# A hybrid encoder layer with retrieved experts: stores moved to ScalarE's queue, a quota of gathered rows, and norms in parts

## The chip, the cores and the metric

One core of a Trainium2 chip runs the whole kernel as one program. The metric is device time in microseconds (us), the median of several executions; less is better. Times inside an execution come from one that was profiled.

## What is computed

One layer works on 1024 tokens of 1024 features. A mixer (an RG-LRU group and an S5 group side by side) is followed by a retrieval of experts, and this second half is what the change touches. The reference, cut to that half:

```python
q = (xb @ wq).reshape(128, 8, 256)              # per block of 128 tokens, 8 heads
s1, s2 = q[..., :128] @ k1.T, q[..., 128:] @ k2.T
v1, i1 = top_k(s1, 16); v2, i2 = top_k(s2, 16)
sc, cidx = top_k((v1[..., :, None] + v2[..., None, :]).reshape(128, 8, 256), 16)
e = i1[cidx // 16] * 128 + i2[cidx % 16]        # 128 experts of 16384 for each token
g = softmax(sc)
act = gelu(einsum('thkd,td->thk', u_tab[e], xb))
out = einsum('thk,thkd->td', g * act, v_tab[e])
h = h + out;  result = rms_norm(h, normf_g)
```

## The kernel before

Of the eight blocks of 128 tokens, three are *gathered* and five are *dense*.

For a **gathered block** (`gather`), each token's 128 expert rows are fetched by an indirect DMA that GpSimd issues. One instruction of VectorE handles one fetched row tile of 128 x 1024: 128 times a product with the block's input `xg` (u rows, which give `act`), then 128 times a multiply and add into `hb` (v rows). Three blocks make 768 rows. Eight row buffers (`rows`) hold what was fetched ahead. A block ends with `finish`, the final norm.

For the **dense blocks** every expert is used with a weight that is mostly zero. `build_g` makes those weights for one block after another: it selects the block's candidates (`topk`), then, in 32 groups of four tokens, multiplies one-hot matrices `ohA` and `ohB` on TensorE and copies the product into `gs` on ScalarE. Every eight groups a store of 2 MB puts `gs` into DRAM (`G_d`). `ahead` makes at the same time 97 of 128 tiles of first-layer activations: load `ur`, split it into a high part `uh` (ScalarE) and a low part `ul` (VectorE), 48 matmuls, Gelu into `aa`, a store into `A_d`. A planner (`Merge.run`) chooses by costs of its own which of these threads writes its next instructions; a scheduler then sets the order on each engine. The engines follow that order strictly. Rows are paced by `PACE`, the planner's us between two.

The **dense schedule** (`dense`) is written out by hand: 32 chunks of four expert tiles (`JC`). In each it makes one more first-layer tile (`first`, 48 matmuls), weighs the activations `hr` and `ha` by the weights (`gt` loaded, `gq` on ScalarE), splits them and the expert rows `vr`, and multiplies into five blocks' sums: 24 matmuls each for blocks 0 to 3 into PSUM pairs (`pair`, two buffers) that `add` takes into `acc`, and block 4 into `total`. `rows_of` places the gathered rows that are left into seven slots of a chunk. `last` does the last chunk's blocks 1 to 4 and their `finish`.

All loads and stores named here are issued by the SP queue, in order, except the row fetches.

Of the kernel before, what the change touches and what calls it, by code (L numbers as in the profile page):

```python
# [844 lines left out]
PACE = 2.0  # L845


def peer(tc, a, cst, pools, h, ss, mg):
# [220 lines left out]
    def build_g(b):  # L1069
# [13 lines left out]
        def flush():  # L1083
# [3 lines left out]
            if t4 % GT == GT - 4:  # L1087
                t0 = b * P + t4 + 4 - GT
                nc.sync.dma_start(G_d[:, :, t0:t0 + GT].rearrange("j p t q -> p j (t q)"),
                                  gs.rearrange("p j t q -> p j (t q)"))  # L1090
                mg.dma(GT * 64)
# [51 lines left out]
    def gate():  # L1143
        return (lambda: mg.units < share[0]) if share else None

    def gather(n):

        xg = gp.tile([P, D], F32, name="xg", tag="xg", bufs=1)
        nc.sync.dma_start(xg, X_d[n])
        act = gp.tile([P, P], F32, name="act", tag="act", bufs=1)  # L1150
        for k in range(P):
# [3 lines left out]
            mg.units += 1  # L1155
        hb = gp.tile([P, D], F32, name="hb", tag="hb", bufs=1)
# [10 lines left out]
        finish(ND + n, hb)  # L1167
        yield

    def finish(b, x):  # L1170
        sq = rows.tile([P, D], F32, name="sqf", tag="row")
        nf = rows.tile([P, D], F32, name="nf", tag="row")
        nc.sync.dma_start(nf, a["gf"].partition_broadcast(P))
        st = gp.tile([P, 3], F32, name="st", tag="st")
        S.activation(sq, x, AF.Square, accum_out=st[:, 0:1])
        rsqrt_cols(mg, st[:, 1:2], st[:, 2:3], st[:, 0:1], 1.0 / D)
        V.scalar_tensor_tensor(x, x, st[:, 2:3], nf, ALU.mult, ALU.mult)
        nc.sync.dma_start(out_v[:, b], x)
# [90 lines left out]
    mg.run([], until="ahead")  # L1269
    pools.close("pk2", "ppt")  # L1270
# [8 lines left out]
    share[:] = [0.0]  # L1279
# [102 lines left out]
    def split_u(c):  # L1382
        uh = pu.tile([P, 8, P], F32R, tag="uh", name="uh")
        ul = pu.tile([P, 8, P], F32R, tag="ul", name="ul")
        split_to(uh, ul, raw_u.pop(c))
        return uh, ul

    def dense():
# [26 lines left out]
        u = split_u(1)  # L1415
        load_v(1, 0)
        carry = None
        for c in range(nch):
# [5 lines left out]
            if more:  # L1424
# [3 lines left out]
                next(fs)  # L1428
            if carry:
                add(*carry)  # L1430
# [11 lines left out]
            if c + 2 < nch:  # L1442
                u = split_u(c + 2)
# [9 lines left out]
            if not more:  # L1453
                finish(0, acc[0])
# [41 lines left out]
    def last(now, pr):  # L1496

        for b in (2, 3, 4):
            p_ = pair() if b < 4 else total
            for jj, t in enumerate(now):  # L1500
                second(p_, b, t, b < 4 and jj == 0, jj == JC - 1)
            if b == 2:
                add(1, pr[1])
                finish(1, acc[1])
            else:
                add(b - 1, p0)
                finish(b - 1, acc[b - 1])
            p0 = p_
        add(4, total)
        finish(4, acc[4])  # L1510
# [84 lines left out]
```

## Time and profile before

| | us |
|---|---|
| median of 3 runs | 2805.51 (2804.67 to 2807.54) |
| the profiled execution | 2802.4 |
| its span, first to last instruction | 2800.6 |
| mean granted TensorE clock, share of full speed | 0.957 |

The span lies 1.8 us inside the profiled execution's time. The program has these stages by the trace: the mixer to about 430 us; queries and first selections to about 700; weights, first-layer tiles and rows to 1657; the dense schedule to about 2740; the last chunk and the norms to the end.

### The profile page before, as it was taken

The numbers are of one execution on the slowest core, as the hardware profiler recorded it, in microseconds if no ns is written. First come the engines' busy times: TensorE is split into PE (matmuls) and PEld (weight loads), VectorE is DVE, ScalarE is ACT, GpSimd is POOL, SyncE is SP. The second block draws the span as 40 slices with busy tenths as digits, with TensorE's granted clock in tenths as the row PEclk, the third lists the DMA queues.
The fourth block names the chain that finished last, engine by engine and source line by source line (L and its number), as shares of the span: only waits on it lengthen the run. The fifth ranks groups of instructions, "written<-read, shape, count | busy, mean of one in ns | idle before, by whom it ended". The sixth has DMA issues, their size and how long they took to land.

```text
span 2800.6 us, 40982 instructions
## 1 busy us (share of the span) xinstructions
PE 2557.1 (91%) x14719; PEld 2308.3 (82%) x14719; DVE 2359.7 (84%) x4536; ACT 1321.8 (47%) x2401; POOL 1145.1 (41%) x777
## 2 busy tenths in 40 slices
PE   6888899888899999999989949999989999999997
PEld 5765688888799899998989848888878888888885
DVE  7786535599999999989989838989988888899996
ACT  5355524322286583864846823344343334443332
POOL 0000000033274474865836624444545554455540
PEclk9998899999999999999999979999999999999998
DMA  4110315466699899998998988999888999999994
GB/s 165 26 30 25 125 56 175 131 225 198 234 356 392 289 385 334 329 399 284 394 328 304 400 293 295 326 327 331 324 300 324 337 330 328 334 335 325 328 334 135
DMA packets 302413, 762.50 MB, mean 272 GB/s; under 512 B 28801, under 2 KB 126401, under 8 KB 297089
## 3 DMA queue, kind: packets, MB, share of 16 engines
q0 software_dynamic: 110592, 402.70, 40.1%
q1 hardware_dynamic: 184736, 345.85, 35.2%
q10 hardware_dynamic: 6880, 11.33, 1.2%
q8 instruction: 116, 1.90, 0.3%
q14 instruction: 89, 0.72, 0.1%
HBM read 669.14 MB, written 89.46 MB: 271 GB/s over the span
## 4 chain that ended last, share of the span: by engine, by line
PE 57%; DVE 21%; DMA 11%; ACT 7%; issue 4%; ACTq 0%; SPq 0%; DVEq 0%
PE vp L146 24%; PE ap L146 12%; PE total L146 6%; DMA A_d<-aa 5%; ACT ohB L146 4%; PE qp L146 4%; DVE row L146 3%; PE wop L146 3%; DVE ix L146 2%; DVE oh L146 2%; DVE ul L146 2%; DVE v L146 2%; PE gp L146 2%; DMA ur<-in_uT_dram 2%; DVE hb L146 1%
## 5 line engine op out<-in xcount | busy, mean ns | idle before, releaser
L1128 POOL DMA_INDIRECT row<-in_peer_u_dram,idx x384 | 564.5, 1470 | 1045.5 <-DVE ix L146 549.6
L1128 POOL DMA_INDIRECT row<-in_peer_v_dram,idx x384 | 577.8, 1505 | 508.0 <-DVE hb L146 392.2
L146 PE MATMUL ap<-xDl,uh 128*128 128x320 f32 x2048 | 655.1, 320 | 42.8 <-ACT aa L146 21.6
L146 PE MATMUL ap<-xDh,ul 128*128 128x320 f32 x2048 | 649.7, 317 | 18.2 <-DVE ul L146 18.2
L146 PE MATMUL ap<-xDh,uh 128*128 128x320 f32 x2048 | 646.4, 316 | 0.0
L146 DVE SCALAR_TENSOR_TENSOR hb<-row,act,hb 128x1024 f32<-128x1024 f32 x384 | 491.7, 1281 | 7.8 <-DMA hb<-H_d 2.7
L146 DVE CUSTOM_DVE_ANT_0 row<-row,xg 128x1024 f32<-128x1024 f32 x384 | 458.6, 1218 | 6.0 <-DMA xg<-X_d 5.0
L146 PEld LDWEIGHTS ap<-xDl,uh 128*128 128x128 f32 x2048 | 392.0, 191 | 46.0 <-ACT aa L146 23.2
L146 PE MATMUL vp<-vl,hh 128*128 128x512 f32 x1024 | 400.3, 391 | 12.3 <-DVE h L146 10.0
L146 PEld LDWEIGHTS ap<-xDh,ul 128*128 128x128 f32 x2048 | 392.1, 191 | 23.0 <-DVE ul L146 21.6
L146 PE MATMUL vp<-vh,hl 128*128 128x512 f32 x1024 | 400.0, 391 | 0.0
L146 PE MATMUL vp<-vh,hh 128*128 128x512 f32 x1024 | 399.9, 391 | 0.0
L146 PEld LDWEIGHTS ap<-xDh,uh 128*128 128x128 f32 x2048 | 391.5, 191 | 0.0
L146 ACT ACTIVATE gq<-gt 128x640 f32<-128x640 f32 x128 | 175.1, 1368 | 352.0 <-DVE hr L146 334.1
L146 DVE TENSOR_TENSOR ul<-ur,uh 128x1024 fp32r<-128x1024 f32 x128 | 155.9, 1219 | 111.1 <-ACT uh L146 110.9
L146 PE MATMUL gp<-ohB,ohA 128*128 128x128 f32 x1280 | 211.8, 284 | 40.6 <-ACT gs L146 19.6
L146 PEld LDWEIGHTS vp<-vl,hh 128*128 128x128 f32 x1024 | 192.9, 188 | 53.9 <-DVE h L146 11.7
L146 PEld LDWEIGHTS gp<-ohB,ohA 128*128 128x128 f32 x1280 | 186.2, 194 | 51.6 <-ACT ohB L146 25.3
L146 PEld LDWEIGHTS vp<-vh,hh 128*128 128x128 f32 x1024 | 192.9, 188 | 40.4
L146 PEld LDWEIGHTS vp<-vh,hl 128*128 128x128 f32 x1024 | 192.9, 188 | 39.3
L146 ACT ACTIVATE aa<-ap 128x320 f32<-128x320 f32 x194 | 85.4, 442 | 276.2 <-PE ap L146 252.5
L146 ACT ACTIVATE ohB<-ohB,kt 128x128 f32<-128x128 f32 x480 | 205.4, 509 | 0.0
(419 smaller groups left out, 4545.8 us busy)
## 6 DMA issues: line engine op xcount, KB each, us to landing
ur<-in_uT_dram SPq DMA_DIRECT2D x128, 512.0 KB, 6.8
vr<-in_peer_v_dram SPq DMA_DIRECT2D x128, 512.0 KB, 6.5
G_d<-gs SPq DMA_DIRECT2D x20, 2048.0 KB, 26.8
gt<-G_d SPq DMA_DIRECT2D x32, 1280.0 KB, 9.8
A_d<-aa SPq DMA_DIRECT2D x97, 320.0 KB, 7.9
hr<-A_d SPq DMA_DIRECT2D x96, 320.0 KB, 5.8
wqr<-in_wq_dram SPq DMA_DIRECT2D x32, 512.0 KB, 4.1
S_d<-sc SPq DMA_DIRECT2D x64, 128.0 KB, 3.9
```

The source lines that it names most:

```text
L146: return fn(*args, **kw)
L1128: G.indirect_dma_start(out=r, out_offset=None, in_=a["peer_v" if at >= P else "peer_u"], in_offset=bass.IndirectOffsetOnAxis(ap=idx[n][:, ...
```

## The change

1. The weights' stores are issued by ScalarE instead of SP.
2. `PACE` is 2.2 instead of 2.0, and the rows stop at a `QUOTA` of 370 until the dense schedule begins. Before, 389 rows are done by then, so the dense schedule now holds 398 instead of 379.
3. The next gathered block's input `xg` is loaded as soon as this block's u rows are done, no longer at the next block's start.
4. `finish` comes in two parts, the squares and the scaling. For a gathered block, one row of the next block lies between them. In the tail the weights `nf` of the norm are loaded once for all five dense blocks, and a block's squares come before the scaling of the block ahead of it. Before, each block loaded its own and was normed in one go.
5. In a chunk, the copy `uh` of the tile for the next chunk but one is written before the second half of this chunk's activations instead of after the first block's matmuls (`high_u`); the difference `ul` stays where it was (`low_u`).

```diff
-PACE = 2.0
+PACE, QUOTA = 2.2, 370
...
-                nc.sync.dma_start(G_d[:, :, t0:t0 + GT].rearrange("j p t q -> p j (t q)"),
-                                  gs.rearrange("p j t q -> p j (t q)"))
+                nc.scalar.dma_start(G_d[:, :, t0:t0 + GT].rearrange("j p t q -> p j (t q)"),
+                                    gs.rearrange("p j t q -> p j (t q)"))
...
     def gate():
-        return (lambda: mg.units < share[0]) if share else None
+        return (lambda: mg.units < share[0]) if share else (lambda: mg.units < QUOTA)
+
+    xgs, pending = [], []
+
+    def load_x(n):
+        if n < NG:
+            xgs.append(gp.tile([P, D], F32, name="xg", tag="xg", bufs=1))
+            nc.sync.dma_start(xgs[n], X_d[n])
...
-        xg = gp.tile([P, D], F32, name="xg", tag="xg", bufs=1)
-        nc.sync.dma_start(xg, X_d[n])
+        if n == 0:
+            load_x(0)
+        xg = xgs[n]
...
             mg.units += 1
+            if pending:
+                pending.pop(0)()
+        load_x(n + 1)
...
-        finish(ND + n, hb)
-        yield
-
-    def finish(b, x):
-        sq = rows.tile([P, D], F32, name="sqf", tag="row")
+        pending.extend(finish(ND + n, hb, last_norm()))
+        pending.pop(0)()
+        yield
+
+    def last_norm():
         nf = rows.tile([P, D], F32, name="nf", tag="row")
         nc.sync.dma_start(nf, a["gf"].partition_broadcast(P))
-        st = gp.tile([P, 3], F32, name="st", tag="st")
-        S.activation(sq, x, AF.Square, accum_out=st[:, 0:1])
-        rsqrt_cols(mg, st[:, 1:2], st[:, 2:3], st[:, 0:1], 1.0 / D)
-        V.scalar_tensor_tensor(x, x, st[:, 2:3], nf, ALU.mult, ALU.mult)
-        nc.sync.dma_start(out_v[:, b], x)
+        return nf
+
+    def finish(b, x, nf):
+
+        st = gp.tile([P, 3], F32, name="st", tag="st", bufs=3)
+
+        def squares():
+            sq = rows.tile([P, D], F32, name="sqf", tag="row")
+            S.activation(sq, x, AF.Square, accum_out=st[:, 0:1])
+
+        def scaled():
+            rsqrt_cols(mg, st[:, 1:2], st[:, 2:3], st[:, 0:1], 1.0 / D)
+            V.scalar_tensor_tensor(x, x, st[:, 2:3], nf, ALU.mult, ALU.mult)
+            nc.sync.dma_start(out_v[:, b], x)
+        return [squares, scaled]
...
     mg.run([], until="ahead")
+    share[:] = [2 * NG * P]
...
-    share[:] = [0.0]
...
+            if c + 2 < nch:
+                uh = high_u(c + 2)
             if carry:
                 add(*carry)
...
             if c + 2 < nch:
-                u = split_u(c + 2)
+                u = low_u(c + 2, uh)
...
     def last(now, pr):
 
-        for b in (2, 3, 4):
-            p_ = pair() if b < 4 else total
+        while pending:
+            pending.pop(0)()
+        nf = last_norm()
+        parts = [finish(b, acc[b], nf) for b in range(ND)]
+        parts[0][0]()
+        p0 = pr[1]
+        for b in range(2, ND):
+            p_ = pair() if b < ND - 1 else total
             for jj, t in enumerate(now):
...
+            add(b - 1, p0)
+            parts[b - 1][0]()
+            parts[b - 2][1]()
             p0 = p_
-        add(4, total)
-        finish(4, acc[4])
+        parts[ND - 2][1]()
+        add(ND - 1, total)
+        parts[ND - 1][0]()
+        parts[ND - 1][1]()
```

How this moves instructions is seen in three places.

The SP queue before, in the third dense block's build: two of its stores (`G_d`) with the stores of first-layer activations (`A_d`) and the loads of expert tiles (`ur`) between them.

```order
L1089 DMA G_d_3227<-gs_11315 128x32x128
L1221 DMA A_d_3226<-aa_11575 128x640
L1183 DMA ur_12050<-in_uT_dram 128x1024
L1221 DMA A_d_3226<-aa_11700 128x640
L1183 DMA ur_12151<-in_uT_dram 128x1024
L1221 DMA A_d_3226<-aa_11823 128x640
L1183 DMA ur_12257<-in_uT_dram 128x1024
L1089 DMA G_d_3227<-gs_11663 128x32x128
```

ScalarE now, at the same store: the copies into `gs`, the store, and the one-hot matrices of the next group behind it.

```order
L146 ACTIVATE gs_11296<-gp_11599 128x4x32x4
L146 ACTIVATE aa_11559<-ap_11619 128x320
L1089 DMA G_d_3227<-gs_11296 128x32x128
L146 ACTIVATE ohB_11671<-iota_63,kt_10633 128x128 x3
L146 ACTIVATE ohB_11671<-ohB_11671,kt_10633 128x128 x3
L146 ACTIVATE uh_11712<-ur_11710 128x1024
```

The store stands between ScalarE's activations, and on SP only `A_d` and `ur` are left.

VectorE in the last dense block's build, before: the groups' one-hot matrices, a tile's low part `ul`, and gathered rows (`row,act<-row,xg`) between them.

```order
L146 TENSOR_TENSOR ul_15475<-ur_15472,uh_15474 128x1024
L146 TENSOR_TENSOR ohA_15536<-iota_63,kt_14760 128x512
L146 TENSOR_SCALAR ohB_15537<-iota_63,kt_14760 128x128
L146 ISA row_15383,act_12803<-row_15383,xg_12801 128x1024
L146 ISA act_12803 128x1
L146 TENSOR_TENSOR ohA_15559<-iota_63,kt_14760 128x512
L146 TENSOR_SCALAR ohB_15560<-iota_63,kt_14760 128x128
L146 ISA row_15422,act_12803<-row_15422,xg_12801 128x1024
```

VectorE in the same build now.

```order
L146 TENSOR_TENSOR ul_15064<-ur_15061,uh_15063 128x1024
L146 TENSOR_TENSOR ohA_15126<-iota_63,kt_14724 128x512
L146 TENSOR_SCALAR ohB_15127<-iota_63,kt_14724 128x128
L146 TENSOR_TENSOR ohA_15146<-iota_63,kt_14724 128x512
L146 TENSOR_SCALAR ohB_15147<-iota_63,kt_14724 128x128
L146 TENSOR_TENSOR ohA_15201<-iota_63,kt_14724 128x512
L146 TENSOR_SCALAR ohB_15202<-iota_63,kt_14724 128x128
L146 TENSOR_TENSOR ohA_15249<-iota_63,kt_14724 128x512
```

The rows between the groups are gone: this build and what follows it to the dense schedule hold 2 rows, and 61 before.

VectorE in the dense schedule where the second gathered block ends and the third begins, before: the last v row, the norm's small steps on `st`, its scaling, and the next block's first u row.

```order
L146 SCALAR_TENSOR_TENSOR hb_16273<-row_19128,act_12803,hb_16273 128x1024
L146 TENSOR_SCALAR st_19371<-st_19371 128x1
L146 RECIPROCAL st_19371<-st_19371 128x1
L146 TENSOR_TENSOR st_19371<-st_19371 128x1 x2
L146 TENSOR_SCALAR st_19371<-st_19371 128x1
L146 TENSOR_TENSOR st_19371<-st_19371 128x1
L146 SCALAR_TENSOR_TENSOR hb_16273<-hb_16273,st_19371,nf_19369 128x1024
L146 ISA row_19146,act_19384<-row_19146,xg_19382 128x1024
```

The same place now.

```order
L146 SCALAR_TENSOR_TENSOR hb_16700<-row_19377,act_12965,hb_16700 128x1024
L146 ISA row_19395,act_19622<-row_19395,xg_16698 128x1024
L146 ISA act_19622 128x1
L146 TENSOR_SCALAR st_19619<-st_19619 128x1
L146 RECIPROCAL st_19619<-st_19619 128x1
L146 TENSOR_TENSOR st_19619<-st_19619 128x1 x2
```

A u row of the third block has moved in between the last v row and the norm's steps, and the scaling follows further on.

## Rows read from the trace of the kernel before

**Rows 1.** The page's part 1: busy time of each engine, its share of the span, and its instructions.

```profile
PE 2557.1 (91%) x14719; PEld 2308.3 (82%) x14719; DVE 2359.7 (84%) x4536; ACT 1321.8 (47%) x2401; POOL 1145.1 (41%) x777
```

**Rows 2.** The busy time of each engine in stretches: bounds and length in us, then for each engine us busy and (instructions), then TensorE's granted clock as a share of full speed, the mean busy share of the 16 DMA engines, and GB/s. First the first four blocks' builds with the gaps behind them, then the first build, the gap behind it, and the last build.

```profile
778.50:1502.10 723.60, 673.79 (x4650) 660.66 (x4650) 685.84 (x1667) 469.41 (x1143) 439.80 (x280) 0.97 0.96 346
778.50:879.80 101.30, 94.84 (x667) 92.09 (x667) 94.58 (x172) 92.35 (x245) 72.59 (x50) 0.98 1.01 377
879.80:958.10 78.30, 73.84 (x505) 72.75 (x504) 78.30 (x282) 25.41 (x48) 27.71 (x23) 1.00 0.92 325
1502.10:1602.80 100.70, 93.99 (x672) 92.32 (x671) 92.86 (x169) 90.45 (x240) 71.27 (x49) 0.97 1.01 376
```

**Rows 3.** VectorE's waits from 778.5 to 1502.1 us: what waited, for what, us in total, times, the longest.

```profile
DVE ul L146 <- ACT uh L146: 28.0, 7, 11.0
DVE ohA L146 <- PE gp L146: 9.4, 4, 4.7
```

**Rows 4.** The SP queue in order of time around two of the weights' stores: start us, us, queue, line, DMA. The us are those that the issue itself takes.

```profile
1005.63 0.37 SPq L1089 DMA_DIRECT2D G_d<-gs  x1
1013.15 16.58 SPq L1221 DMA_DIRECT2D A_d<-aa  x1
1032.48 0.43 SPq L1089 DMA_DIRECT2D G_d<-gs  x1
1033.01 17.33 SPq L1221 DMA_DIRECT2D A_d<-aa  x1
```

**Rows 5.** The source line of the weights' stores: their count and the issue's ns (least, median, most), first and last start; then us from issue to landing.

```profile
L1089 SPq DMA_DIRECT2D G_d<-gs x20: 370/371/2082, 802.8 to 1611.3; - x20
DMA to landing us min/median/max: 16.7/26.8/37.7
```

**Rows 6.** ScalarE's own queue in the front part: seven loads that it issues, and the activation behind them.

```profile
284.58 7.25 ACTq L796 DMA_DIRECT2D h<-in_x_dram  x7
291.88 0.63 ACT L146 ACTIVATE wgh<-wg 128x512 fp32r<-128x512 f32 x1 [6.25 <-DMA wor<-in_w_out_dram]
```

**Rows 7.** VectorE in order of time, two gathered rows of the u kind one behind the other; then the page's part 5 for rows of the v and the u kind (count, us busy, mean ns).

```profile
1593.45 1.22 DVE L146 CUSTOM_DVE_ANT_0 row<-row,xg 128x1024 f32<-128x1024 f32 x1
1594.59 1.22 DVE L146 CUSTOM_DVE_ANT_0 row<-row,xg 128x1024 f32<-128x1024 f32 x1
L146 DVE SCALAR_TENSOR_TENSOR hb<-row,act,hb 128x1024 f32<-128x1024 f32 x384 | 491.7, 1281 | 7.8 <-DMA hb<-H_d 2.7
L146 DVE CUSTOM_DVE_ANT_0 row<-row,xg 128x1024 f32<-128x1024 f32 x384 | 458.6, 1218 | 6.0 <-DMA xg<-X_d 5.0
```

**Rows 8.** ScalarE, the SP queue and VectorE in order of time from the last copy of weights to the first product of the dense schedule.

```profile
1610.65 0.60 ACT L146 ACTIVATE gs<-gp 128x512 f32<-128x512 f32 x1 [0.45 <-PE gp L146]
1611.28 0.37 SPq L1089 DMA_DIRECT2D G_d<-gs  x1
1636.67 0.32 SPq L1265 DMA_DIRECT2D gt<-G_d  x1
1642.88 1.33 ACT L146 ACTIVATE gq<-gt 128x640 f32<-128x640 f32 x1 [17.70 <-DMA gt<-G_d]
1657.73 0.82 DVE L146 TENSOR_TENSOR hr<-hr,gq 128x640 f32<-128x640 f32 x1 [33.87 <-DMA hr<-A_d]
```

**Rows 9.** The chain of waits in the dense schedule, the start of three chunks one behind another (start us, us, what), and the busy time in the whole dense schedule and in one chunk.

```profile
1984.72 7.03 PE ap L146 x48
2019.00 7.04 PE ap L146 x48
2064.16 7.03 PE ap L146 x48
1676.00:2740.00 1064.00, 1055.68 (x5160) 909.64 (x5160) 946.17 (x1021) 423.39 (x463) 536.68 (x368) 0.99 0.91 325
1984.70:2019.00 34.30, 34.30 (x171) 29.57 (x170) 31.13 (x31) 13.81 (x15) 18.91 (x12) 1.00 0.89 319
```

**Rows 10.** VectorE in order of time in the chunk that begins at 2019.00, those instructions that it waited before, and TensorE's wait in the same chunk.

```profile
2027.49 1.23 DVE L146 TENSOR_TENSOR ul<-ur,uh 128x1024 fp32r<-128x1024 f32 x1 [2.96 <-ACT uh L146]
2032.64 0.16 DVE L146 RECIPROCAL st<-st 128x1 f32<-128x1 f32 x1 [1.36 <-ACT st L146]
2034.26 1.29 DVE L146 SCALAR_TENSOR_TENSOR hb<-hb,st,nf 128x1024 f32<-128x1024 f32 x1 [0.69 <-DMA nf<-in_gf_dram]
2040.54 1.22 DVE L146 CUSTOM_DVE_ANT_0 row<-row,xg 128x1024 f32<-128x1024 f32 x1 [4.99 <-DMA xg<-X_d]
2045.25 0.79 PE L146 MATMUL vp<-vl,hh 128*128 128x512 f32 x1 [8.30 <-DVE h L146]
```

**Rows 11.** VectorE's waits in the dense schedule, two of them.

```profile
DVE ul L146 <- ACT uh L146: 76.5, 29, 8.4
DVE hb L146 <- DMA hb<-H_d: 2.7, 1, 2.7
```

**Rows 12.** The tail: TensorE's last matmul, and three of VectorE's five scalings of a block.

```profile
2783.54 0.39 PE L146 MATMUL total<-vh,hh 128*128 128x512 f32 x1
2770.29 1.28 DVE L146 SCALAR_TENSOR_TENSOR h<-h,st,nf 128x1024 f32<-128x1024 f32 x1 [1.16 <-DMA nf<-in_gf_dram]
2776.80 1.28 DVE L146 SCALAR_TENSOR_TENSOR h<-h,st,nf 128x1024 f32<-128x1024 f32 x1 [1.48 <-DMA nf<-in_gf_dram]
2795.79 1.28 DVE L146 SCALAR_TENSOR_TENSOR h<-h,st,nf 128x1024 f32<-128x1024 f32 x1 [1.37 <-DMA nf<-in_gf_dram]
```

More of the change, by code (lines that the diff above doesn't have):

```diff
@@ L1380, in load_u, with high_u, low_u @@
             nc.sync.dma_start(raw_u[c], a["uT"][tile(c, 2).j])
-    def split_u(c):
+    def high_u(c):
         uh = pu.tile([P, 8, P], F32R, tag="uh", name="uh")
+        S.activation(uh, raw_u[c], AF.Copy)
+        return uh
+    def low_u(c, uh):
         ul = pu.tile([P, 8, P], F32R, tag="ul", name="ul")
-        split_to(uh, ul, raw_u.pop(c))
+        V.tensor_tensor(ul, raw_u.pop(c), uh.bitcast(F32), ALU.subtract)
         return uh, ul
@@ L1414, in dense @@
         weights(1)
-        u = split_u(1)
+        u = low_u(1, high_u(1))
         load_v(1, 0)
@@ L1452, in dense @@
             add(0, pr[0])
-            if not more:
-                finish(0, acc[0])
             rows_of(2)
@@ L1496, in last @@
     def last(now, pr):
-        for b in (2, 3, 4):
-            p_ = pair() if b < 4 else total
-            for jj, t in enumerate(now):
[L1501 to L1507, printed above, removed]
+        while pending:
[6 more added lines that the diff above has]
+            p_ = pair() if b < ND - 1 else total
+            for jj, t in enumerate(now):
+                second(p_, b, t, b < ND - 1 and jj == 0, jj == JC - 1)
+            add(b - 1, p0)
+            parts[b - 1][0]()
+            parts[b - 2][1]()
             p0 = p_
-        add(4, total)
-        finish(4, acc[4])
+        parts[ND - 2][1]()
+        add(ND - 1, total)
+        parts[ND - 1][0]()
+        parts[ND - 1][1]()
     with tc.manual_schedule():
```

## The prediction

> **What bounds the kernel now.** I read the page first, then the stretches by stage, then the waits in each. Over the span TensorE and VectorE are both near full [rows 1], so the average says little. By stage there are three regimes.
>
> From about 700 to 1645 us the kernel does three things at once. It makes the weights of five blocks; I call a *build* the 32 groups of one block, and a *gap* the selection of the next block's candidates up to its first group. It makes 97 tiles of first-layer activations, and it works off gathered rows. In a build the DMA engines are full (share 1.01, 377 GB/s) while VectorE has 6.7 us idle of 101.3. In a gap VectorE has none: 78.30 of 78.30 [rows 2]. Over the first four builds and gaps it is busy 685.8 of 723.6 us. Of the 37.8 idle, 28.0 is a `ul` waiting for its `uh`, and 9.4 a group waiting for TensorE [rows 3]. The `uh` is late because its transfer is: behind a weights' store the SP queue's next issue stands 16.58 and 17.33 us, and the tile loads stand behind that [rows 4].
>
> The dense schedule, 1676 to about 2740, belongs to TensorE. A chunk takes 34.3 us, TensorE is busy in all of it, and VectorE in 31.1 [rows 9]. One chunk stands out: from 2019.00 to 2064.16, 45.2 us.
>
> The tail is serial: the last block's norm ends 13.1 us after the last matmul [rows 12].
>
> **The change part by part.** *Pace and quota.* Rows finished before the dense schedule fall from 389 to 370. A plain reading saves 19 rows of VectorE, 22 us. The order says otherwise. Counted over the whole order, builds one to four and their gaps hold 49, 21, 47, 22, 48, 22, 47, 22 rows before (278) and 53, 29, 42, 33, 40, 41, 35, 45 now (318). The last build with what follows holds 61 before and 2 now. So the quota is used up before the last build, in which VectorE then has 32 groups and its tile splits and stands idle, and the four stages in which it was the fullest engine get 40 rows more. A row starts 1.14 us after the one before; a row of the v kind is 0.06 longer [rows 7], so I take 1.17. 40 x 1.17 = 46.8, and one `ul` less (1.14) makes 45.7. VectorE's work there becomes 685.8 + 45.7 = 731.5 us against 723.6 elapsed: longer by at least 8 even with no idle.
>
> *The stores on ScalarE.* What the SP queue lost behind a store is gone, so the tiles' loads come in time and I take the 28.0 us of waits on `uh` away. The 9.4 us stay: 740.9. If nothing of the 28.0 goes, it is 769. The issue itself now costs ScalarE its own time: 0.37 us each as on SP, 2.08 at the most [rows 5]. ScalarE was busy 92.35 of 101.3 us in a build [rows 2], so four issues (1.5 us, at most 8.3) fit into 9 us; without that cover they would be 7.4 us over all twenty.
>
> The rows are now bunched, too. The fourth gap has 45 rows (0.524 MB each), 9 tiles (0.852 MB in and out) and one store (2.1 MB): 33.3 MB, or 29.7 less the seven rows fetched ahead. At a build's 377 GB/s that is 79 us, and VectorE's 45 x 1.17 + 9 x 1.14 make 63. The third gap misses 7 in the same way. Bounds 0 and 23; I take 4, nearer to nothing, since the builds ahead of these gaps now move less than they could. Stages one to four: 745 us, **+21** (bounds +8 and +68).
>
> *The last build and the hand-over.* The last build is no longer VectorE's nor the DMA's, but TensorE was busy 93.99 of its 100.7 us [rows 2] with nine tiles in it, and now there are ten (7.03 us each [rows 9]), so little can go: -2 (bounds -4 and +5). The hand-over took 46.5 us, from the end of the last `gs` (1611.25) to the first `hr` (1657.73): the store 25.4 until the load of `gt` could start, then 6.2 to `gq`, then the copies behind `gq` on ScalarE, the last half tile and its way through DRAM [rows 8]. Now no row transfers lie beside the store: I take 16.7, the shortest landing seen [rows 5], -8.7. It starts behind one more `aa` copy, +2, and four copies instead of three stand behind `gq`, half a tile more, +3.5. Together -3 (bounds -8 and +5). Last build and hand-over: **-5**.
>
> *Next block's input ahead, norms in parts.* In the slow chunk VectorE waits for `uh`, then through the norm for ScalarE's squares and root, then for `nf`, then 5.0 us for `xg`; the add that frees a PSUM pair comes late and TensorE stands 8.30 us [rows 10]. Now `xg` has been there for 128 rows, a gathered row lies between squares and root, and `uh` is early; what is left, the root (1.36) and up to 1 us for `nf`, is well inside what the add has: it came 8.3 us late after 11 us of waits, so some 3 us pass unseen. The chunk falls back to 34.3: -10.9. On the other side the quota moves the change from u to v of the second block into the dense schedule. Its `hb` load stands on the SP queue behind the next `xg` load, and VectorE will wait for it; the same wait later is 2.7 us [rows 11], inside VectorE's 3.2 idle of a chunk, so I take +1 (up to +5). **-10**.
>
> *Late tile copied first.* `uh` is copied between the two halves of the activations. This takes away most of 76.5 us of VectorE idle in the dense schedule [rows 11], but TensorE did not wait for it: 0, with TensorE's 34.3 as cover. The same cover hides the 19 more rows (22 us over 31 chunks, 0.7 each, against 3.2 idle); without it they cost 22.
>
> *The tail.* Before, each block's cycle is 6.2 to 6.5 us, held by its own load of `nf`. Now `nf` is loaded once, squares go ahead of the earlier block's scaling, and TensorE's 24 matmuls of a block set the pace (5.4 us: a chunk without its 7.03 is 27.3 for 120). Following the new order with the old durations: last rows one row later (+1.2), scalings that end at about 2772.5 (that block's `nf` still follows the store of the gathered block), 2777.4, 2782.3 and 2784.9, and the last near 2790 against 2797.07: **-7** (bounds -4 and -9).
>
> **The sum.** +21 - 5 - 10 - 7 = -1. The profiled execution took 2802.4 us (span 2800.6), 3 us under the median of the runs, 2805.5; at the median's level the new kernel takes about **2804 us**: no change that can be measured (0.2%, 5.6 us, is about what a measurement of this kernel can tell).
>
> **The rivals.** *The store frees nobody* (slower, from the point at which less than about 20 of the 28 us go). The builds run at 377 GB/s with the engines full; what the tile loads lose to a store on their own queue they may lose to the same bytes on another. Then the 28.0 us stay, stages one to four cost +49, and the sum is +27: 2832; with half of it, 2818. For it: the share of 1.01 and tile loads that land late in every build. Against it: the SP issue itself stands still for 17 us, and three of four builds now carry 5 to 12 rows less.
> The Trainium skill (DMA: Bandwidth & Descriptors, section "Issuing engines are not separate DMA queues") says that starting DMAs from several engines saves only the sequencer's issue time, since all run on the same 16 engines. By that rule alone this rival would be right and the time 2832; the trace agrees in the full share and differs in the 17 us, which are sequencer time and far from small.
>
> *The last build runs free* (faster). If VectorE's idle vanishes altogether in the first four stages (+8), and the last store, alone on its queue and with no rows beside it, lands at once and lets the hand-over end at TensorE's own pace (-14 with the last build), the sum is 8 - 14 - 10 - 7 = -23: 2782. For it: TensorE has 4.5 tiles left after the last group, 32 us, and 46.5 pass. Against it: the chain store, load, copies, tile, store, load stays in series.
>
> *ScalarE held by the issue.* ScalarE's seven loads of `h` took 7.25 us to issue and its next activation began only at their end [rows 6], so an issue is ScalarE's own time. If the store holds it as long as SP's next issue stood, 17 us, twenty of them are 340 us, less 2.5 us each of slack: 3094. Against it: the stores' own issues read 0.37 on SP. It decides from 2.5 us an issue.
>
> *The dense wait moves.* If the early second block's `hb` or the split norm makes an add late, 8 of the 10 us come back: 2812.
>
> **How the numbers follow.** The sum with its own spread of 8 us: 0.46 (of it 0.14 faster, 0.27 same, 0.05 slower). The last build runs free: 0.25. The store frees nobody, wholly or by half: 0.18. ScalarE held: 0.04. The dense wait moves: 0.07 (0.04 same, 0.03 slower). Faster 0.39, same 0.31, slower 0.30. The range reaches to the free last build below and nearly to the whole 28 us above, 2782 to 2829; the likeliest case's own is 2796 to 2812.
>
> **What would show it.** The first four builds and gaps take 735 to 755 us instead of 723.6, with VectorE busy about 731; no wait of `ul` on `uh` over a few us there; a last build with VectorE under half busy; the first `hr` 10 to 20 us later than 1657.7. No chunk over 36 us in the dense schedule, though its rows are 398. A last scaling some 10 us after the last matmul or less. I am wrong if the stores do not free SP (waits on `uh` as before), if the first four stages end no later than now, or if a chunk other than the old one grows.

## The result and the profile after

The changed kernel takes **2837.99 us** (median of 4 runs, 2835.85 to 2842.74), against 2806.53 us (2804.67 to 2811.03) for the kernel before in the same comparison: ratio 1.0112, 95% interval 1.0093 to 1.0131. It is slower by 31 us. The prediction was no change, 2804, with a range to 2829. The profiled execution took 2842.7 us (span 2841.0), 40.4 more in span than the one before; it was the slowest of the four, so differences by stage below add up to more than 31.

The page of the changed kernel: part 1, and two rows of part 2 (busy tenths of VectorE and of the DMA engines, 40 slices of 71 us).

```profile
PE 2579.3 (91%) x14719; PEld 2332.9 (82%) x14719; DVE 2366.1 (83%) x4536; ACT 1327.0 (47%) x2401; POOL 1101.5 (39%) x777
DVE  7787535599999999998997427999989999899997
DMA  5010315366698998999889557999999999899994
```

The totals hardly moved against [rows 1]; VectorE has 6 us more. The slices show where they lie: in slices 23 and 24 (1562 to 1705 us), the last build and the hand-over, VectorE falls to 4 and 2 tenths and the DMA engines to 5 and 5. In the ten slices ahead of that both are at 8 or 9, but for VectorE's 7 in the last of them, which lies in the fourth gap.

The stretches of the changed kernel (columns as in [rows 2]): the first four builds and gaps together, the first build, the third gap, the fourth gap, the last build.

```profile
783.40:1560.60 777.20, 688.47 (x4616) 677.16 (x4615) 733.30 (x1744) 472.36 (x1137) 463.35 (x318) 0.93 0.95 345
783.40:904.80 121.40, 98.79 (x667) 96.22 (x667) 113.14 (x274) 92.53 (x242) 78.02 (x55) 0.90 0.96 355
1281.00:1360.90 79.90, 71.06 (x448) 70.00 (x446) 67.26 (x103) 25.64 (x42) 60.08 (x40) 0.91 1.00 380
1481.30:1560.60 79.30, 67.49 (x446) 66.16 (x444) 64.16 (x105) 22.03 (x38) 63.81 (x44) 0.97 1.03 400
1560.60:1663.40 102.80, 100.52 (x725) 100.26 (x726) 44.32 (x79) 95.09 (x248) 5.90 (x5) 0.97 0.56 185
```

The first four stages grew from 723.6 to 777.2 us. In them VectorE is busy 733.3 us, which is what the prediction had (731.5). But 43.9 us of idle stand beside it, where 13 were forecast. (Before, 37.8 stood there, so most of what the stages grew by is VectorE's added work, 47.5 us.) In the last build VectorE is busy 44.3 of 102.8 us, and the build is no shorter for it.

VectorE's waits in the first four stages of the changed kernel (columns as in [rows 3]).

```profile
DVE row L146 <- DMA row<-in_peer_u_dram,idx: 26.5, 30, 1.5
DVE ohA L146 <- PE gp L146: 8.1, 7, 4.2
DVE row L146 <- issue: 4.3, 2, 3.3
DVE hb L146 <- DMA row<-in_peer_v_dram,idx: 2.6, 1, 2.6
DVE ul L146 <- ACT uh L146: 0.7, 3, 0.3
```

The wait of `ul` for `uh`, 28.0 us in [rows 3], is gone, as forecast. A new one has its size: rows that wait for their own transfer, 26.5 us in 30 pieces. With 4.3 us where GpSimd's issue came late and 2.6 for v rows that makes 33.4. Of these, 27.8 lie in the third and fourth gaps.

Two other things changed in these stages. The copies into `gs`, which never waited for a store before, now do:

```profile
ACT gs L146 <- DMA G_d<-gs: 26.5, 4, 13.0
```

And TensorE's granted clock is 0.93 on average there, 0.97 before. Both would reach VectorE as a wait for TensorE's products. That wait is 8.1 us here (and 1.3 more for TensorE's first-layer work), and it was 9.4 before, so neither shows as a cause of the longer stages.

ScalarE and VectorE from the last copy of weights to the first product of the dense schedule, in the changed kernel.

```profile
1668.29 0.60 ACT L146 ACTIVATE gs<-gp 128x512 f32<-128x512 f32 x1 [1.31 <-PE gp L146]
1668.91 0.37 ACTq L1089 DMA_DIRECT2D G_d<-gs  x1
1702.64 0.83 DVE L146 TENSOR_TENSOR hr<-hr,gq 128x640 f32<-128x640 f32 x1 [21.15 <-DMA hr<-A_d]
```

From the end of the last `gs` (1668.88) to the first `hr` (1702.64) are 33.8 us; it was 46.5 [rows 8].

The dense schedule of the changed kernel: its stretch; VectorE's wait for `hb` in it; one of the two such waits; TensorE's waits in the same chunk.

```profile
1702.60:2829.40 1126.80, 1097.87 (x5326) 943.82 (x5327) 1017.77 (x1120) 449.53 (x498) 558.14 (x390) 0.99 0.89 323
DVE hb L146 <- DMA hb<-H_d: 13.9, 2, 7.0
1769.43 2.60 DVE L146 SCALAR_TENSOR_TENSOR hb<-row,act,hb 128x1024 f32<-128x1024 f32 x2 [7.03 <-DMA hb<-H_d]
1775.87 0.50 PE L146 MATMUL vp<-vl,hh 128*128 128x512 f32 x1 [2.47 <-DVE h L146]
1780.88 0.50 PE L146 MATMUL vp<-vl,hh 128*128 128x512 f32 x1 [2.00 <-DVE h L146]
```

From the first product of block 4 to that of the next chunk the old slow chunk took 44.1 us (45.2 by its first tile, [rows 9]) and takes 36.8 now. But two other places grew. Where a block goes from u rows to v rows VectorE stands 7.0 us for `hb`, and TensorE waits for the adds behind it: two chunks there take 75.2 us instead of 68.6, and later two take 72.8.

TensorE's last matmul and VectorE's last scaling in the changed kernel.

```profile
2829.64 0.39 PE L146 MATMUL total<-vh,hh 128*128 128x512 f32 x1
2835.86 1.28 DVE L146 SCALAR_TENSOR_TENSOR h<-h,st,nf 128x1024 f32<-128x1024 f32 x1
```

The norm ends 7.5 us after the last matmul starts, against 13.5 [rows 12].

By stage (us; from first group to first group, so that the four stages before read 722.8; the tail from the last matmul's start):

| | first group starts | stages 1 to 4 | last build and hand-over | first `hr` to last matmul | tail |
|---|---|---|---|---|---|
| before | 778.5 | 722.8 | 156.4 | 1125.8 | 13.5 |
| after | 783.4 | 777.2 | 142.0 | 1127.0 | 7.5 |
| difference | +4.9 | **+54.4** | **-14.4** | +1.2 | -6.0 |

The first column is not the change's: nothing before it was edited to take time, and in the twelve kernels below it lies between 777.2 and 786.5 where that part is in the scheduler's order (the two in written order: 804 and 805).

### The profile page after: what moved, and what is told of

Read it like the earlier page. It is cut to its first block, busy times and chain, and to the rows that moved or that the text cites. A ratio compares the mean times of both kernels' runs of the same rounds, so it can differ in the third digit from the quotient of the medians.

```text
span 2841.0 us, 40982 instructions
## 1 busy us (share of the span) xinstructions
PE 2579.3 (91%) x14719; PEld 2332.9 (82%) x14719; DVE 2366.1 (83%) x4536; ACT 1327.0 (47%) x2401; POOL 1101.5 (39%) x777
## 5 line engine op out<-in xcount | busy, mean ns | idle before, releaser
L1128 POOL DMA_INDIRECT row<-in_peer_u_dram,idx x384 | 536.3, 1397 | 1185.8 <-PE qp L146 542.2
L1128 POOL DMA_INDIRECT row<-in_peer_v_dram,idx x384 | 562.3, 1464 | 461.8 <-DVE hb L146 322.8
L146 PE MATMUL ap<-xDh,ul 128*128 128x320 f32 x2048 | 662.2, 323 | 53.3 <-DVE ul L146 49.8
L146 PE MATMUL ap<-xDl,uh 128*128 128x320 f32 x2048 | 664.0, 324 | 30.1 <-ACT uh L146 20.2
L146 PE MATMUL ap<-xDh,uh 128*128 128x320 f32 x2048 | 655.6, 320 | 0.0
L146 DVE SCALAR_TENSOR_TENSOR hb<-row,act,hb 128x1024 f32<-128x1024 f32 x384 | 491.5, 1280 | 20.9 <-DMA hb<-H_d 13.9
L146 PEld LDWEIGHTS ap<-xDh,ul 128*128 128x128 f32 x2048 | 400.2, 195 | 60.1 <-DVE ul L146 58.9
L146 PEld LDWEIGHTS ap<-xDh,uh 128*128 128x128 f32 x2048 | 399.4, 195 | 0.0
L146 PE MATMUL gp<-ohB,ohA 128*128 128x128 f32 x1280 | 220.3, 288 | 42.7 <-DVE ohB L146 23.4
L146 PEld LDWEIGHTS gp<-ohB,ohA 128*128 128x128 f32 x1280 | 198.1, 201 | 49.5 <-issue 19.5
L146 PEld LDWEIGHTS vp<-vl,hh 128*128 128x128 f32 x1024 | 193.2, 189 | 54.4 <-DVE h L146 12.4
L146 PEld LDWEIGHTS vp<-vh,hh 128*128 128x128 f32 x1024 | 192.9, 188 | 40.4
L146 DVE TENSOR_TENSOR h<-h,vp 128x1024 f32<-128x1024 f32 x128 | 155.8, 1217 | 49.2 <-PE vp L146 49.0
```

Source lines behind the costliest of these rows:

```text
L146: return fn(*args, **kw)
L1128: G.indirect_dma_start(out=r, out_offset=None, in_=a["peer_v" if at >= P else "peer_u"], in_offset=bass.IndirectOffsetOnAxis(ap=idx[n][:, ...
```

## Experiments

Each kernel's ratio is to the kernel before on the same chip, in brackets its 95% interval. VectorE's order is given by its rows in build, gap, build, gap and so on; before: 49, 21, 47, 22, 48, 22, 47, 22, and 61 in the last build and behind it; after: 53, 29, 42, 33, 40, 41, 35, 45, and 2.

### One part at a time

**The stores alone** (`e1_stores`), on the kernel before:

```diff
-                nc.sync.dma_start(G_d[:, :, t0:t0 + GT]
+                nc.scalar.dma_start(G_d[:, :, t0:t0 + GT]
```

> The kernel before with the twenty stores of the weights begun by ScalarE and nothing else changed. Theory 1 (the stores' new engine changes the order on VectorE: 27, 30, 39 and 43 rows in the four gaps instead of 21, 23, 23 and 22, the next block's selection in the builds): the first four builds and gaps end 45 to 60 us later than before (723.6), with 20 to 40 us of VectorE idle on arriving rows, the hand-over is some 10 us shorter, and the kernel is slower by 30 to 45 us, about 2840. Theory 2 (the pace and the quota of rows did it; the stores alone only free the SP queue): faster by 15 to 30 us, about 2780.

**Pace and quota alone** (`e2_rows`), on the kernel before:

```diff
-PACE = 2.0
+PACE, QUOTA = 2.2, 370
...
-        return (lambda: mg.units < share[0]) if share else None
+        return (lambda: mg.units < share[0]) if share else (lambda: mg.units < QUOTA)
```

> The kernel before with the pace of 2.2 and the quota of 370 rows, and nothing else changed; the stores stay on SP. Theory 1 (the stores' engine made the new order): the gaps hold 19 to 21 rows, the order of the first four stages stays as before, they take 705 to 725 us, and the kernel is faster by 0 to 15 us, 2790 to 2805. Theory 2 (pace and quota bunch the rows and starve the last build): slower by 20 us or more, 2825 or over.

**The edits of the dense schedule and the tail alone** (`e3_dense`): the changed kernel with the stores on `nc.sync`, `PACE = 2.0` and no quota.

> The kernel before with the edits of the dense schedule and the tail alone (late tile copied first, norms in parts, next block's input ahead); stores on SP, pace 2.0, no quota. Both theories: the front part as before to within 5 us. The tail gives 6 us. With 389 rows ahead the second block goes from u to v before the dense schedule, so only the third block's wait for its hb is left, 4 us, and the old slow chunk gives back 7 to 11: faster by 9 to 13 us, about 2795. If the dense edits are worth nothing (what the slow chunk loses comes back elsewhere), about 2800.

**All but pace and quota** (`e4_no_rows`): the changed kernel with `PACE = 2.0` and no quota.

> The changed kernel with pace 2.0 and without the quota: stores on ScalarE, dense edits, 389 rows ahead. Theory 1 (the stores' engine): no better than the changed kernel within 10 us, 2828 to 2848. Theory 2 (pace and quota): the gain of stores and dense edits together, 2770 to 2790.

| | median, us | ratio | stages 1 to 4 | last build and hand-over | dense |
|---|---|---|---|---|---|
| stores alone | 2850.16 | 1.0157 (1.0127 to 1.0188) | 774.9 | 140.4 | 1126.3 |
| pace and quota alone | 2787.71 | 0.9926 (0.9900 to 0.9952) | 702.9 | 145.0 | 1141.2 |
| dense and tail alone | 2789.71 | 0.9925 (0.9896 to 0.9953) | 722.1 | 155.8 | 1114.9 |
| all but pace and quota | 2830.65 | 1.0074 (1.0046 to 1.0101) | | | 1112.4 |

(In the last one the fifth block's first group stands only 14 us behind the fourth build, so the cut by groups doesn't fall where it does in the others.)

Stores alone: the four stages, then VectorE's waits in them.

```profile
784.60:1559.50 774.90, 682.94 (x4616) 672.76 (x4614) 736.19 (x1749) 471.89 (x1137) 475.37 (x319) 0.94 0.95 348
DVE row L146 <- DMA row<-in_peer_u_dram,idx: 24.6, 30, 4.0
DVE ul L146 <- ACT uh L146: 0.6, 1, 0.6
```

Pace and quota alone: the same.

```profile
783.50:1486.40 702.90, 666.73 (x4642) 658.22 (x4642) 677.07 (x1651) 467.84 (x1139) 421.22 (x272) 0.98 0.97 349
DVE ul L146 <- ACT uh L146: 12.0, 6, 5.0
DVE ohA L146 <- PE gp L146: 13.6, 8, 5.9
```

Theory 2, which was the prediction's own (the quota bunches the rows and empties the last build), fell. The stores on ScalarE do it alone. Their order is 55, 27, 46, 30, 42, 39, 38, 43, and 19 behind, with the selection of the next block written into the builds; the quota then takes most of what is left for the last build. Pace and quota with the stores on SP leave the order nearly as it was (49, 19, 45, 21, 46, 21, 50, 20, and 49), take 9 us of VectorE's work and 16 of its waits on `uh` out of the four stages, and gain 20 us, though the dense schedule is 15 longer with them. Of the 42 us that the stores cost, 52 lie in the four stages (VectorE 736.2 busy instead of 685.8; 24.6 waiting for rows stand where 28.0 on `uh` stood), 16 come back in the last build and the hand-over, and 6 lie ahead of the change. The dense edits gain more than expected, 18 us by the medians; the profile has 11 in the dense schedule and 4 in the tail.

The parts do not add up: 42 - 20 - 18 would be 4, and the change costs 31. Stores and dense edits do add up (22.5 measured, 24 by the parts). What does not add up is pace and quota: they gain 20 us with the stores on SP, and with the stores on ScalarE they cost some 10 (1.0112 with them, 1.0074 without, intervals that overlap a little). The stretches show why: from the first group to the first `hr` of the changed kernel, then the same and the dense schedule without pace and quota.

```profile
783.40:1702.60 919.20, 820.28 (x5544) 808.19 (x5543) 781.29 (x1825) 578.03 (x1404) 469.24 (x322) 0.94 0.89 320
784.80:1702.90 918.10, 816.19 (x5545) 804.07 (x5543) 804.42 (x1859) 579.27 (x1405) 493.62 (x341) 0.94 0.92 333
1702.90:2815.30 1112.40, 1092.42 (x5328) 940.51 (x5328) 994.15 (x1081) 449.13 (x497) 526.52 (x371) 0.99 0.88 318
```

With the stores on ScalarE, 19 rows less ahead of the dense schedule bring nothing there (919.2 and 918.1 us): the rows that pace and quota take away are those of a last build in which VectorE has time. The cost is in the dense schedule, 1126.8 us with them and 1112.4 without. It is there with the stores on SP as well, 1141.2 against 1125.8 for the kernel before, where the gain ahead of it is larger. With the quota, the second gathered block goes from u to v rows inside the dense schedule; VectorE waits for `hb` twice there, 13.9 us, and once, 3.2, without.

### Is it the queue or the order?

**Stores begun by GpSimd** (`e5_pool`): `nc.gpsimd.dma_start(G_d...`, on the kernel before. The order on VectorE stays nearly that of before.

> The kernel before with the twenty stores begun by GpSimd instead of SP. VectorE's order stays nearly that of before (47, 46, 47, 47 rows in the builds and 23, 23, 23, 22 in the gaps). Theory 1a (a store on another queue than SP is good; what costs is the order that comes with ScalarE): the 28 us of ul waiting for uh shrink under 8, the first four builds and gaps take 695 to 715 us, 2780 to 2800. Theory 1b (a store off SP is itself the cost, since its bytes now lie beside the tiles' loads or the gs buffers come free late): no gain or slower, 2808 to 2845. A third way: GpSimd's issue holds up the gathered rows behind it; then VectorE waits for rows, and the gain is gone too.

2811.34 us, ratio 1.0027 (1.0009 to 1.0046). The four stages and three of VectorE's waits in them:

```profile
779.00:1511.20 732.20, 680.45 (x4640) 667.75 (x4639) 686.67 (x1666) 470.64 (x1139) 455.63 (x295) 0.97 0.94 341
DVE row L146 <- DMA row<-in_peer_u_dram,idx: 20.7, 9, 6.7
DVE hb L146 <- DMA row<-in_peer_v_dram,idx: 19.6, 10, 4.8
DVE ul L146 <- ACT uh L146: 1.1, 1, 1.1
```

Then, in order of time, a store issued by GpSimd and the wait on VectorE behind it, twice:

```profile
989.75 1.74 POOL L1089 DMA_DIRECT2D G_d<-gs  x1
1006.51 1.29 DVE L146 SCALAR_TENSOR_TENSOR hb<-row,act,hb 128x1024 f32<-128x1024 f32 x1 [4.37 <-DMA row<-in_peer_v_dram,idx]
1017.11 1.74 POOL L1089 DMA_DIRECT2D G_d<-gs  x1
1034.02 1.28 DVE L146 SCALAR_TENSOR_TENSOR hb<-row,act,hb 128x1024 f32<-128x1024 f32 x1 [3.40 <-DMA row<-in_peer_v_dram,idx]
```

This is the third way of the expectation, with a turn. The wait on `uh` fell from 28.0 to 1.1 us, but VectorE waits 40.3 us for rows, and the longest of these waits end 16 to 18 us after a store was issued, 16.8 and 16.9 in these rows. That is about the time by which the SP queue's next issue stood still before: 16.58 and 17.33 us [rows 4], and 9.7 to 20.4 behind the twenty stores. In the changed kernel no issue on SP takes 5 us in these stages. So what comes next in the queue that holds a store waits for it: tile loads on SP, gathered rows on GpSimd. The issue itself is also dearer there, 1.74 us instead of 0.37. The run changes more than the queue, though: by part 3 of the pages GpSimd's stores go in 10560 packets, and in 82240 for the same bytes from SP or ScalarE.

**Written order, stores on SP and on ScalarE** (`e7_written_sp`, `e8_written_act`). From the first build to the last tile the scheduler is switched off, so that the engines follow the planner's order; VectorE, TensorE and GpSimd then have the same rows in both kernels.

```diff
     mg.add([(0.0, build()), (1.0, ahead())])
+    fixed = ExitStack()
+    fixed.enter_context(tc.manual_schedule())
     mg.run([], until="k")
...
     mg.run([], until="ahead")
+    fixed.close()
```

> The kernel before, from the first build to the last tile of activations in the written order of the program (no reordering of instructions there); stores on SP. Only a base for the next run: 51 to 52 rows in each build, 18 to 19 in each gap, the selection all in the gaps. Somewhere between 2790 and 2850. Waits of ul on uh behind the stores as in the kernel before, 20 us or more.

> As the run in written order, but the stores begun by ScalarE. The order of VectorE, TensorE and GpSimd is the same row for row, so the difference of the two is that of the queue alone. Theory 1a (the order made the loss): faster than the run with SP by 5 to 30 us. Theory 1b (a store on ScalarE costs by itself: gs copies that wait for a store that lands late, 26 to 41 us in the runs so far): slower than it by 15 us or more.

3500.29 us with SP, 3464.50 with ScalarE. The ranges do not overlap (3496.63 to 3505.51, 3461.43 to 3467.01). VectorE's wait in the four stages, first with SP, then with ScalarE:

```profile
DVE ul L146 <- ACT uh L146: 537.4, 59, 18.1
```

```profile
DVE ul L146 <- ACT uh L146: 496.9, 59, 14.6
```

The same four stages, first with SP, then with ScalarE:

```profile
805.00:2098.80 1293.80, 802.87 (x4680) 782.84 (x4679) 736.78 (x1665) 480.04 (x1141) 371.26 (x279) 0.78 0.59 194
803.80:2057.40 1253.60, 807.16 (x4680) 786.89 (x4679) 737.12 (x1666) 480.10 (x1141) 370.11 (x279) 0.80 0.61 200
```

With the order held, the stores on ScalarE are worth 36 us (5 to 30 were expected), and the wait of `ul` is 40 us shorter. So in this order the queue is not the cost. But this order is not the scheduler's. The kernel with SP was expected at 2790 to 2850 us and both are far slower, with builds of 200 us and the DMA engines busy 0.59 and 0.61 of the time. So the 36 us are not what a tuned order would gain, and the pair does not show what a store on ScalarE's queue costs where the DMA engines are full; no copy into `gs` waits for a store here. For the scheduler's order the changed kernel's own rows speak: the wait on `uh` is gone, the wait for TensorE has not grown, and the 47.5 us of added work are the order's. Whether the rows' waits of 33.4 us come from the order alone stays open, since no run holds the scheduler's order with the stores on ScalarE.

The Trainium skill (DMA: Bandwidth & Descriptors, section "Issuing engines are not separate DMA queues") has it that starting DMAs on several engines saves sequencer time alone. Here the trace bears out half of it: on GpSimd the wait only changed its victim. In the written order the other queue was worth 36 us, and 17 us for which an issue stands behind a store is sequencer time that is not small.

### What the rows cost, and where

**Stores back on SP** (`e6_on_sp`): the changed kernel with `nc.sync` for the stores.

> The changed kernel with the stores back on SP: pace 2.2, quota 370 and the dense edits. Theory 1: the gains of the rows alone (20 us) and of the dense edits alone (18 us), less what both took from the same slow chunk (up to 11): 2770 to 2785. Theory 2 (pace and quota cost): 2805 or over.

2772.27 us, ratio 0.9886 (0.9863 to 0.9910). So without the stores' new engine the change is worth 1.1%, of the 1.5% that its two other parts give one by one. Within the changed kernel the engine of the stores costs 66 us by the medians. The stretch from the first group to the first `hr` takes 853.2 us with the stores on SP and 919.2 with them on ScalarE, while VectorE has nearly the same work in it, 775.5 and 781.3 us: what differs is where that work lies.

**Forty rows less in the last build** (`e9_quota330`): stores on SP, `QUOTA` 330.

> The changed kernel with the stores on SP and the quota 330 instead of 370: the first four builds and gaps keep their rows (49, 19, 45, 21, 46, 21, 49, 19), the last build has 11 instead of 51. Theory 1 (rows in the last build cost next to nothing, because TensorE and the DMA engines set its length, and rows in the first four stages cost their full VectorE time): the last build shrinks by no more than 6 us from 107 though VectorE loses 47 us of work in it, the hand-over by no more than 5, and the 40 rows more in the dense schedule (1.5 us a chunk of 34.3) cost 0 to 12: within 8 us of the same kernel with 370, 2765 to 2780. If VectorE's rows set the last build, it shrinks by 30 us or more: under 2750.

2764.74 us, ratio 0.9851 (0.9821 to 0.9881). The last build of the run before, then the last build and the dense schedule of this one:

```profile
1487.20:1594.40 107.20, 99.86 (x718) 99.70 (x718) 97.75 (x177) 93.94 (x244) 80.37 (x53) 0.96 1.01 371
```

```profile
1488.20:1584.50 96.30, 96.30 (x712) 95.94 (x711) 54.02 (x97) 93.29 (x244) 18.14 (x13) 1.00 0.71 234
1623.30:2750.30 1127.00, 1098.83 (x5328) 943.66 (x5328) 1059.72 (x1198) 450.09 (x498) 623.36 (x430) 0.99 0.93 342
```

The build shrank by 10.9 us, more than the 6 expected, while VectorE lost 43.7 us of work in it: a row costs 0.27 us there, against the 1.17 of VectorE's time that it takes. TensorE is busy in all of the 96.30. The dense schedule took the 40 rows for nothing (1127.5 and 1127.0 us).

**Thirty-eight rows less in the fourth gap** (`e10_act330`): the changed kernel, stores on ScalarE, `QUOTA` 330.

> The changed kernel with the quota 330, stores on ScalarE: the fourth gap has 7 rows instead of 45, all stages ahead of it as in the changed kernel. Theory 1 (in the fourth gap VectorE waits for rows that the DMA engines bring too slowly): that gap shrinks from 79.3 to TensorE's own 67 to 70 and no row is waited for in it; the other stages stay; the dense schedule takes the 38 rows at 0 to 12 us: 2820 to 2838. If something else than the rows holds that gap (the stores' queue, TensorE), it stays at 77 to 80.

2826.20 us, ratio 1.0068 (1.0040 to 1.0095): 12 us better than the change by the medians. The fourth gap:

```profile
1480.70:1542.80 62.10, 62.10 (x429) 62.09 (x428) 20.49 (x28) 21.89 (x38) 9.93 (x7) 1.00 0.67 236
```

It went from 79.3 to 62.1 us, further than expected, and TensorE is busy in all 62.1. The rows held it, at 0.45 us each: below that TensorE sets the length.

**Half a row fetched for each index** (`e12_half`), on the changed kernel. The index now counts half rows, so the fetched addresses lie in the first half of each table, and the other half of what a row needs is left out:

```diff
-        G.indirect_dma_start(out=r, out_offset=None, in_=a["peer_v" if at >= P else "peer_u"],
+        G.indirect_dma_start(out=r[:, :D // 2], out_offset=None,
+                             in_=a["peer_v" if at >= P else "peer_u"].rearrange("n (a d) -> (n a) d", a=2),
```

> The changed kernel with half of each gathered row fetched (2 KB instead of 4 KB for each of 128 addresses); VectorE then works twice on the half for a row of the u kind, so that a row costs it 0.1 to 0.2 us more, and reads the half twice for a row of the v kind. Part of the computation is left out. Theory 1 (the waits on rows are the DMA engines' bytes): the waits of rows on their transfers in the first four stages fall from 29 us under 8, and the fourth gap from 79 to 70 to 74. If the rows come late for another reason (the number of addresses, GpSimd's own issue), the fourth gap stays at 78 or over with VectorE idle in it.

2800.23 us, ratio 0.9973 (0.9954 to 0.9992). The four stages, the fourth gap, and the longest of VectorE's waits in the four stages:

```profile
777.20:1521.60 744.40, 680.30 (x4661) 671.30 (x4659) 739.11 (x2105) 475.55 (x1141) 410.80 (x312) 0.96 0.77 249
1452.30:1521.50 69.20, 67.25 (x461) 66.72 (x459) 69.19 (x201) 22.85 (x38) 49.22 (x45) 1.00 0.93 313
DVE ohA L146 <- PE gp L146: 3.8, 5, 1.8
```

No row is waited for any more. The four stages take 744.4 us, though VectorE has 6 us more to do in them than in the changed kernel; the fourth gap falls from 79.3 to 69.2 us and VectorE is busy in all of it, the third from 79.9 to 64.3. So the wait goes with the bytes of the rows. GpSimd's issues show the same: a fetch in the fourth gap of the changed kernel, then here (count, us busy, mean ns, idle before).

```profile
L1128 POOL DMA_INDIRECT row<-in_peer_u_dram,idx x44 | 65.5, 1488 | 16.3 <-issue 11.6 <-DVE act L146 2.9 <-DMA row<-in_peer_u_dram,idx 1.8
```

```profile
L1128 POOL DMA_INDIRECT row<-in_peer_u_dram,idx x45 | 49.2, 1094 | 20.3 <-DVE act L146 10.0 <-issue 9.8 <-DVE ul L146 0.3
```

The same number of addresses takes 1.09 us to issue instead of 1.49 when half the bytes follow. In the changed kernel GpSimd issues with little pause in this gap, 65.5 us of 79.3, so its issues may pace the rows as well as the transfers do; the run does not part the two.

### The wait for hb

**`hb` loaded behind the seventeenth u row** (`e11_hb`), stores on SP:

```diff
             if pending:
                 pending.pop(0)()
+            if k == 16:
+                hb = gp.tile([P, D], F32, name="hb", tag="hb", bufs=1)
+                nc.sync.dma_start(hb, H_d[n])
         load_x(n + 1)
-        hb = gp.tile([P, D], F32, name="hb", tag="hb", bufs=1)
-        nc.sync.dma_start(hb, H_d[n])
```

> The changed kernel with the stores on SP, and the load of a gathered block's hb moved ahead, behind the block's seventeenth row instead of its last row of the u kind. Theory: VectorE's wait for hb (7.0 and 6.9 us in the changed kernel) is gone and the chunks with it (excess of 6.6 and 3.9 us there) go back to 34.3: 5 to 11 us faster than with the stores on SP alone, 2761 to 2768. If hb was not what made those chunks long (the rows of the v kind bunched behind the change from u to v), nothing changes: 2770 to 2775.

2760.90 us, ratio 0.9841 (0.9808 to 0.9874), the lowest median here and faster than both kernels (with the quota 330 as well it was not tried). The interval overlaps that of the stores on SP alone, so the gain of the early load is read from the stage. Its dense schedule:

```profile
1636.70:2750.00 1113.30, 1092.49 (x5328) 940.85 (x5328) 1016.29 (x1118) 449.99 (x498) 551.83 (x390) 0.99 0.90 327
```

1113.3 us against 1127.5 with the late load; of the chunks that were long there one of 36.4 and one of 35.0 remain. VectorE's wait for `hb`, 14.3 us in the dense schedule of the kernel with stores on SP alone, does not appear.

## Why the prediction was wrong

Two terms of its sum failed: the bunched rows, taken at 4 us and measured at 33.4, and the dense schedule, taken at -10 and measured at +1.2.

**VectorE's work in the first four stages: right in size, wrong in cause.** 731.5 us were forecast, 733.3 measured. But the prediction laid the 40 rows more to pace and quota. They come with the stores' new engine: the stores alone bring 736.2, pace and quota alone take 9 away. The size was right because it was counted in the order of the whole change. Had the parts' orders been compared one by one, the cause would have shown before any run.

**The waits on `uh`: right.** 28.0 us became 0.7. The 9.4 us for TensorE became 8.1 and 1.3.

**The bunched rows: this step failed.** The prediction had the bytes of the fourth gap at 79 us and those of the third 7 us over VectorE's work, and then took 4 of its bounds 0 to 23, "since the builds ahead of these gaps now move less than they could". The fourth gap took 79.3 us, with 15.1 of VectorE idle, and the third had 12.6. A build that moves less helps only by what the row buffers hold, and the seven rows fetched ahead were already taken off. The term measured 33.4 us, beyond its own upper bound: 27.8 in these two gaps, the rest in small pieces elsewhere. With half the bytes no row was waited for. (That the stages then took 744.4 us, next to the 745 of the prediction, is chance: VectorE had 6 us more to do in that run.)

**The last build and the hand-over: right in kind, too small.** -5 was taken, -14.4 measured. Of that -12.7 lies in the hand-over, 33.8 us instead of 46.5, where -3 was taken and -8 was the bound. The build up to its last `gs` hardly moved (108.2 us for 110.0), as said. The reason given, no rows beside the last store, fits all the runs: with 13 rows left behind the last build the hand-over takes 42.7 to 49.4 us, with 5 or none 30.0 to 34.3, and on SP with none it is as short (30.0, pace and quota alone) as on ScalarE.

**The dense schedule: this step failed too.** -10 was taken, +1.2 measured. The old chunk gave back 7.3 us, the last one 2.1, but the change from u to v was priced at +1 (up to +5) for VectorE's 3.2 idle of a chunk, and cost 6.6 once and 4 again later. The wait was 7.0 us, not 2.7, and it comes in front of adds that free PSUM. With the stores on SP, loading `hb` earlier took 14 us out of the dense schedule, so this wait is most of what it lost. The rival "the dense wait moves" named this mechanism and had a chance of 0.07. The 19 more rows cost nothing by their work: 40 rows more in the same schedule are free (`e9_quota330`).

**The tail: right**, -6.0 for -7.

The sum of what was measured is +54.4 - 14.4 + 1.2 - 6.0 = +35, and +4.9 of the profile's difference lies ahead of the change; the medians differ by 31.

Of the rivals, "the store frees nobody" came nearest in time (2832), by luck: the store did free the SP queue. With the stores on GpSimd, too, the tiles' loads came in time, and the loss went to the rows behind a store, not to the tiles. Of "the last build runs free" half came: -14.4 us for its -14, but the idle of the first four stages did not go. "ScalarE held by the issue" did not come: the stores' issues took 0.37 to 0.39 us each. Of the prediction's own signs of being wrong one came true: chunks other than the old one grew. The first four stages took 777 us, over the 735 to 755 that would have borne it out.

## What to carry to other kernels

Where a scheduler sets the order, compare it for each part of a change by itself: here one word, the engine that begins twenty stores, moved some 40 rows between stages and cost 42 us, while the same word was worth 36 us in a slower order that was held. Price work by the stage where it lands: taking rows out gained 0.45 us a row in the full fourth gap and 0.27 in the last build, and putting them into the dense schedule cost nothing, though each is 1.17 us of VectorE's time. Price what moves with them too: the second block's change from u to v came along into the dense schedule and made it wait. When a stage's bytes by the measured rate exceed its time, take that time, unless there are buffers to fetch ahead into.

## What the runs showed of the hardware

On SP and on GpSimd a 2 MB store delayed what follows it in its own queue: SP's next issues stood 16.58 and 17.33 us [rows 4] and 9.7 to 20.4 over all twenty stores, and with the stores on GpSimd rows came 16.8 and 16.9 us after the store's issue. On ScalarE nothing but the stores was queued in these stages, so no run shows it there. ScalarE issues such a store in 0.37 us and GpSimd in 1.74. An indirect fetch of 128 rows is not issued in a fixed time: 1.49 us on average in a gap at 400 GB/s, 1.09 where half the bytes follow.
